# Retention gates and output product: 512- and 256-column matmuls into two banks instead of three 256-column matmuls into one

## The chip, the cores and the metric

The kernel runs on one core of a Trainium2 chip. A core has a matrix engine (TensorE, in the profile PE, with PEld for its weight loads), a vector engine (VectorE, DVE), an activation engine (ScalarE, ACT), a general engine (GpSimd, POOL) and a queue that starts transfers (SyncE, SP). Each engine runs its instructions in the order in which they were written out for it, and waits on semaphores for the others. The metric is the device time of one execution in microseconds (us). Three runs of the kernel before gave 1389.72, 1392.71 and 1392.83 us, median 1392.71.

## The reference

A trunk of four layers works on 256 frames of 1024 channels in float32. Layers 0 and 3 mix the frames by retention, layer 1 by a convolution module, layer 2 by stick-breaking attention; each layer ends with a squared-ReLU feed-forward network. The change touches the second half of the retention mixer, which is this (four heads, 512 value channels each):

```python
proj = xn @ w_in
q, k, v, g = jnp.split(proj, [D_MODEL, 2 * D_MODEL, 4 * D_MODEL], axis=-1)
...
y = (y - mu) * lax.rsqrt(var + EPS)
y = y * gn_w + gn_b
return (jax.nn.silu(g) * y) @ w_out
```

The gate g is a 1024 x 2048 product, w_out a 2048 x 1024 one. Both appear in layers 0 and 3.

## The kernel before, in words

**Numbers.** Float32 products are made from two parts: a value is the sum of hi and lo, and a product is taken as hi x hi + hi x lo + lo x hi. Activations lie transposed (channels on the 128 partitions), as tiles of 128 x 512 whose columns 0 to 255 are hi and 256 to 511 lo (S is 256). Helper `split` (L349, L350) makes such a tile: a cast gives hi, a VectorE subtraction gives lo. x itself is kept as four tiles x0 to x3 of 128 x 512.

**Weights.** They stream in as units of 128 x 1024, in the order in which the program uses them. ScalarE casts a unit to `wh` (L337), VectorE subtracts to get `wl` (L338). There are five buffers of each kind, so a unit is cast only when the unit five before it has been used for the last time. A unit holds eight weight tiles of 128 x 128: four contraction steps (kk) times two halves of the output (m).

**Two ways to multiply.** `mm_b` (L457 to L459) issues three matmuls of 256 columns for each weight tile (wh x hi, wh x lo, wl x hi), all into one half of one PSUM bank; two output halves share a bank. `mm_w` (L484, L485) issues one matmul of 512 columns (wh x [hi, lo]) and one of 256 (wl x hi) into a bank of its own for each half. The bank then holds two sums that must still be added: `sum_w` copies one half to SBUF on ScalarE (L507) and adds the other on VectorE (L508). The accumulators `acc` have four banks, and four other banks, `mis`, serve everything small; a tile takes the bank that was free first.

**The retention part.** For each head: the y product into two `mis` banks (L793 to L796), squares on ScalarE (L800), sums on GpSimd, a column sum on TensorE (L374), and a reciprocal root on two columns on VectorE, which gives G. Two gate pairs p = 0, 1 follow (L818): `pair_b` with two units each, a multiplication by the norm's factor (L820) and a SiLU (L822). G is spread over partitions by a TensorE product, `bcast` (L381), copied out of its bank by ScalarE (L385, Gb). Then y is finished for each half e: VectorE multiplies by Gb (L828), ScalarE applies scale and bias twice (L833), VectorE multiplies by the SiLU (L838), and two splits (L349, L350) give two tiles of the output product's input. A scheduler that simulates the engines fixes each engine's order, so that the steps of one head stand among the matmuls of the next.

**The output product.** `res_pairs` computes four output pairs in two groups of two. For each of four contraction units kb (one head each) and each pair it uses one unit; after the last unit a pair is added to x by one VectorE instruction (L851), and its norm parts follow (L404, L405, L415). Group 0 needs head 3's y at its last unit.

## Time and profile before

| what | value |
| --- | --- |
| median of three runs | 1392.71 us (1389.72 to 1392.83) |
| the profiled execution | 1390.83 us |
| its span | 1389.0 us, so 1.83 us lie outside it |
| TensorE busy | 1371.8 us, 8838 matmuls |
| VectorE, ScalarE, GpSimd busy | 1011.7, 794.9, 190.6 us |
| gates of layer 0, output product of layer 0 | 109 to 163 us, 163 to 211 us |
| the same in layer 3 | 1094 to about 1148 us, and on to about 1203 us |

A matmul's row gives its start and its modelled length. Matmuls overlap, so the step from one start to the next says what a matmul costs, and the length does not. The clock of TensorE stands in the column PEclk, 1.00 being full speed.

### The profile page before, as it was taken

To read this page: it belongs to the slowest core of one execution; us is meant where nothing else is said; L and a number is where in the kernel's file an instruction comes from. 1 tells how busy PE (TensorE), PEld (TensorE's weight loads), DVE (VectorE), ACT (ScalarE), POOL (GpSimd) and SP (SyncE) were. 2 spreads that over 40 slices of the span, in tenths; PEclk is the share of its full clock that TensorE was granted. 3 is DMA by queue.
4 is the path that set the end of the run, shared out by engine and by line. 5 is a ranking of instruction groups with operands and counts; after the bars stand their busy time and mean duration, and the time that the engine had idled before them with its cause. 6 is when DMAs were issued, how large, how long until landed. Compare 5 with 4: busy or idle time off the path is not lost.

```text
span 1389.0 us, 22290 instructions
## 1 busy us (share of the span) xinstructions
PE 1371.8 (99%) x8838; PEld 1244.6 (90%) x8838; DVE 1011.7 (73%) x1715; ACT 794.9 (57%) x1203; POOL 190.6 (14%) x189
## 2 busy tenths in 40 slices
PE   9999999999998999999999999999999999999998
PEld 7889998888998888888988898888988999988888
DVE  6967778775779978766578578755597687788643
ACT  7545556664457556654458666654565554555442
POOL 2201102000449820000000010000110010100011
PEclk9999999999999999999999999999999999999999
DMA  8644445555454035555553345555554444555550
GB/s 302 213 166 149 152 158 198 194 183 186 178 182 152 1 109 195 183 186 194 195 176 128 118 155 186 196 195 182 182 182 175 159 151 155 180 184 186 192 193 35
DMA packets 34522, 235.79 MB, mean 170 GB/s; under 512 B 3952, under 2 KB 4592, under 8 KB 6768
## 3 DMA queue, kind: packets, MB, share of 16 engines
q1 hardware_dynamic: 34128, 233.83, 47.3%
q8 instruction: 69, 1.13, 0.3%
q10 hardware_dynamic: 288, 0.52, 0.1%
q14 instruction: 37, 0.30, 0.1%
HBM read 233.29 MB, written 1.05 MB: 169 GB/s over the span
## 4 chain that ended last, share of the span: by engine, by line
PE 95%; DVE 2%; DMA 1%; ACT 1%; issue 0%; POOL 0%; SPq 0%; ACTq 0%; DVEq 0%; POOLq 0%
PE acc L484 31%; PE acc L485 16%; PE acc L459 9%; PE acc L458 9%; PE acc L457 9%; PE acc L874 4%; PE acc L873 4%; PE acc L875 4%; PE acc L969 2%; PE mis L374 1%; DMA raw<-in_w 1%; PE mis L381 1%; DVE wl L338 1%; PE acc L473 1%; PE acc L472 1%; PE acc L471 1%
## 5 line engine op out<-in xcount | busy, mean ns | idle before, releaser
L338 DVE TENSOR_TENSOR wl<-raw,wh 128x1024 fp32r<-128x1024 f32 (+1 forms) x444 | 555.5, 1254 | 284.4 <-ACT wh L337 279.1
L337 ACT CAST wh<-raw 128x1024 fp32r<-128x1024 f32 (+1 forms) x444 | 461.8, 1042 | 421.7 <-PE acc L484 203.1
L484 PE MATMUL acc<-z,wh 128*128 128x512 f32 x1120 | 391.1, 394 | 0.0
L485 PE MATMUL acc<-z,wl 128*128 128x256 f32 x1120 | 313.1, 281 | 0.0
L484 PE MATMUL acc<-big,wh 128*128 128x512 f32 x768 | 267.7, 393 | 0.0
L484 PEld LDWEIGHTS acc<-z,wh 128*128 128x128 f32 x1120 | 209.3, 187 | 47.3
L485 PE MATMUL acc<-big,wl 128*128 128x256 f32 x768 | 215.2, 280 | 0.0
L485 PEld LDWEIGHTS acc<-z,wl 128*128 128x128 f32 x1120 | 211.5, 189 | 0.8
L484 PEld LDWEIGHTS acc<-big,wh 128*128 128x128 f32 x768 | 143.8, 187 | 32.6
L458 PE MATMUL acc<-big,wh 128*128 128x256 f32 x576 | 163.2, 284 | 1.0 <-DVE big L350 1.0
L457 PE MATMUL acc<-big,wh 128*128 128x256 f32 x576 | 162.3, 286 | 1.9 <-DVE big L349 1.9
L459 PE MATMUL acc<-big,wl 128*128 128x256 f32 x576 | 163.2, 284 | 0.0
L459 PE MATMUL acc<-z,wl 128*128 128x256 f32 x512 | 145.2, 284 | 0.5 <-DVE wl L338 0.5
L457 PE MATMUL acc<-z,wh 128*128 128x256 f32 x512 | 145.4, 284 | 0.0
L485 PEld LDWEIGHTS acc<-big,wl 128*128 128x128 f32 x768 | 145.1, 189 | 0.0
L458 PE MATMUL acc<-z,wh 128*128 128x256 f32 x512 | 144.9, 283 | 0.0
L420 POOL TENSOR_TENSOR t<-t,t 128x512 f32<-128x512 f32 x25 | 38.7, 1549 | 735.3 <-DVE z L405 456.9
L457 PEld LDWEIGHTS acc<-big,wh 128*128 128x128 f32 x576 | 110.3, 193 | 2.8 <-DVE big L349 2.4
L458 PEld LDWEIGHTS acc<-big,wh 128*128 128x128 f32 x576 | 111.2, 193 | 1.2 <-DVE big L350 1.2
L459 PEld LDWEIGHTS acc<-big,wl 128*128 128x128 f32 x576 | 111.2, 193 | 0.0
L459 PEld LDWEIGHTS acc<-z,wl 128*128 128x128 f32 x512 | 98.1, 192 | 0.7 <-DVE wl L338 0.7
L458 PEld LDWEIGHTS acc<-z,wh 128*128 128x128 f32 x512 | 98.1, 192 | 0.0
(252 smaller groups left out, 1964.7 us busy)
## 6 DMA issues: line engine op xcount, KB each, us to landing
raw<-in_w SPq DMA_DIRECT2D x216, 1024.0 KB, 4.8
raw<-in_w SPq DMA_DIRECT2D x8, 512.0 KB, 8.5
x<-in_x SPq DMA_DIRECT2D x4, 256.0 KB, 6.2
cst<-in_cst SPq DMA_DIRECT2D x4, 192.0 KB, 4.9
cst<-in_cst SPq DMA_DIRECT2D x1, 532.0 KB, 9.5
out<-t SPq DMA_DIRECT2D x2, 256.0 KB, 2.7
out<-t ACTq DMA_DIRECT2D x2, 256.0 KB, 2.9
prm<-in_prm SPq DMA_DIRECT2D x1, 189.5 KB, 9.3
```

What stands on the lines that cost most here:

```text
L337: nc.scalar.copy(hi[:, s], src[:, s])
L338: nc.vector.tensor_sub(lo[:, s], src[:, s], hi[:, s])
L420: (nc.vector if p == 3 and self.quick else nc.gpsimd).tensor_add(a, self.sq, q)
L457: nc.tensor.matmul(o, wh[:, kk, cs], ah, start=st, stop=False, **kw)
L458: nc.tensor.matmul(o, wh[:, kk, cs], al, start=False, stop=False, **kw)
L459: nc.tensor.matmul(o, wl[:, kk, cs], ah, start=False, stop=en, **kw)
L484: nc.tensor.matmul(ps[m], wh[:, kk, cs], a, start=first and kk == 0, stop=False, **kw)
L485: nc.tensor.matmul(ps[m][:, :S], wl[:, kk, cs], a[:, :S], start=False, stop=last and kk == 3, **kw)
L873: nc.tensor.matmul(ps[t], zh[:, s], wh[:, kk], start=k == 0, stop=False, skip_group_check=True)
L874: nc.tensor.matmul(ps[t], zh[:, s], wl[:, kk], start=False, stop=False, skip_group_check=True)
L875: nc.tensor.matmul(ps[t], zl[:, s], wh[:, kk], start=False, stop=k == 7, skip_group_check=True)
L969: nc.tensor.matmul(o, dgs[t, w], tap(t, w), start=first, stop=last, **kw)
```

## The change

Four things are edited; what they do in layers 0 and 3 is the same.

- Gate pairs go from `pair_b` to `pair_w`: two banks a pair, then `sum_w` (two ScalarE copies, two VectorE additions of 128 x 256), and L820's multiplication reads the sum from SBUF.
- `res_pairs` with group 2, which only the retention layers use, goes over to `mm_w` with two banks for each output pair, for all four pairs. A group of two pairs so holds all four `acc` banks, where it held two. The last unit of a pair is issued half by half (`by_m`). Four VectorE additions of 128 x 256 take the place of one of 128 x 512 for each pair.
- `pair_w` issues the unit kb = 7 half by half; only the feed-forward network's second product has so many.
- Temporaries are reused in place, and the high part of the four y splits of a head is cast by ScalarE where VectorE did it.

There are 32 gate units and 32 output units in the two layers, with eight weight tiles each: 512 weight tiles lose one matmul of three.

```diff
--- before.py
+++ after.py
@@ -473,16 +473,15 @@
                 nc.tensor.matmul(o, wl[:, kk, cs], a[:, :S], start=False, stop=last and kk == 3, **kw)
 
 
-    def mm_w(self, ps, w, acts, k0, first, last):
+    def mm_w(self, ps, w, acts, k0, first, last, by_m=False):
         nc = self.nc
         wh, wl = v3(w[0], 4, 256), v3(w[1], 4, 256)
         kw = dict(skip_group_check=True)
-        for kk in range(4):
+        for kk, m in [(kk, m) for m in range(2) for kk in range(4)] if by_m else [(kk, m) for kk in range(4) for m in range(2)]:
             a = acts(k0 + kk)
-            for m in range(2):
-                cs = slice(m * P, (m + 1) * P)
-                nc.tensor.matmul(ps[m], wh[:, kk, cs], a, start=first and kk == 0, stop=False, **kw)
-                nc.tensor.matmul(ps[m][:, :S], wl[:, kk, cs], a[:, :S], start=False, stop=last and kk == 3, **kw)
+            cs = slice(m * P, (m + 1) * P)
+            nc.tensor.matmul(ps[m], wh[:, kk, cs], a, start=first and kk == 0, stop=False, **kw)
+            nc.tensor.matmul(ps[m][:, :S], wl[:, kk, cs], a[:, :S], start=False, stop=last and kk == 3, **kw)
 
     def pair_b(self, name, l, c0, acts, nkb=2):
         ps = self.acc()
@@ -496,7 +495,7 @@
         ps = [self.acc(), self.acc()]
         for kb in range(nkb):
             w = self.unit((name, l, "b", kb, c0))
-            self.mm_w(ps, w, acts, kb * 4, kb == 0, kb == nkb - 1)
+            self.mm_w(ps, w, acts, kb * 4, kb == 0, kb == nkb - 1, by_m=kb == 7)
         return self.sum_w(ps)
 
     def sum_w(self, ps):
@@ -527,15 +526,20 @@
         return [self.sum_w(ps[0]), self.sum_w(ps[1])]
 
     def res_pairs(self, name, l, acts, nkb, group, evac, before=None):
+        wide = group == 2
         for g in range(4 // group):
-            ps = [self.acc() for _ in range(group)]
+            ps = [[self.acc(), self.acc()] if wide else self.acc() for _ in range(group)]
             for kb in range(nkb):
                 if before is not None:
                     before(kb)
                 for p in range(group):
                     w = self.unit((name, l, "b", kb, (g * group + p) * 256))
-                    self.mm_b(ps[p], w, acts, kb * 4, kb == 0, kb == nkb - 1)
-                    if kb == nkb - 1:
+                    last = kb == nkb - 1
+                    if wide:
+                        self.mm_w(ps[p], w, acts, kb * 4, kb == 0, last, by_m=last)
+                    else:
+                        self.mm_b(ps[p], w, acts, kb * 4, kb == 0, last)
+                    if last:
                         evac(g * group + p, ps[p])
 
 
@@ -799,10 +803,10 @@
                 s = self.tmp()
                 nc.scalar.activation(out=s, in_=yb[e], func=AF.Square)
                 sq.append(s)
-            ss = self.tmp()
-            nc.gpsimd.tensor_add(ss, sq[0], sq[1])
-            sh = self.tmp(S)
-            nc.gpsimd.tensor_add(sh, ss[:, :S], ss[:, S:])
+            ss = sq[0]
+            nc.gpsimd.tensor_add(ss, ss, sq[1])
+            sh = ss[:, :S]
+            nc.gpsimd.tensor_add(sh, sh, ss[:, S:])
             vr = self.mis()
             for t in range(2):
                 self.colsum(vr[:, t : t + 1], sh[:, t * P : (t + 1) * P], self.sc(512))
@@ -815,9 +819,8 @@
             nc.vector.tensor_mul(G, rs, fh)
             sg = []
             for p in range(2):
-                ps = self.pair_b("ret_w_in", j, 4 * D + h * DV + p * 256, self.zs)
-                t = self.tmp()
-                nc.vector.tensor_mul(v3(t, 2, S), v3(ps, 2, S), self.b2(rb))
+                t = self.pair_w("ret_w_in", j, 4 * D + h * DV + p * 256, self.zs)
+                nc.vector.tensor_mul(v3(t, 2, S), v3(t, 2, S), self.b2(rb))
                 s = self.bigt()
                 nc.scalar.activation(out=s, in_=t, func=AF.Silu)
                 sg.append(s)
@@ -826,17 +829,15 @@
             for e in range(2):
                 u = self.tmp()
                 nc.vector.tensor_mul(v3(u, 2, S), v3(yb[e], 2, S), self.b2(Gb))
-                a = self.tmp()
                 for f in range(2):
                     cc = h * 4 + e * 2 + f
                     s = slice(f * S, (f + 1) * S)
                     nc.scalar.activation(
-                        out=a[:, s], in_=u[:, s], func=AF.Identity,
+                        out=u[:, s], in_=u[:, s], func=AF.Identity,
                         scale=self.p(("gw", j), cc), bias=self.p(("gb", j), cc),
                     )
-                pr = self.tmp()
-                nc.vector.tensor_mul(pr, a, sg[e])
-                y += [self.split(pr[:, :S], "dve"), self.split(pr[:, S:], "dve")]
+                nc.vector.tensor_mul(u, u, sg[e])
+                y += [self.split(u[:, :S]), self.split(u[:, S:])]
         self.out_proj("ret_w_out", j, y, 4, 2, nxt)
 
     def out_proj(self, name, l, y, nkb, group, nxt, bias=None, before=None):
@@ -847,7 +848,12 @@
 
         def evac(p, ps):
             x = self.x[p]
-            if bias is None:
+            if isinstance(ps, list):
+                for f in range(2):
+                    s = slice(f * S, (f + 1) * S)
+                    for o in (ps[f][:, :S], ps[f][:, S:]):
+                        nc.vector.tensor_add(x[:, s], o, x[:, s])
+            elif bias is None:
                 nc.vector.tensor_add(x, ps, x)
             else:
                 for f in range(2):
```

Line numbers rise by a few after the edit: `mm_w` is L483 and L484 there, `sum_w` L506 and L507, the y product L797 to L800, the squares L804, the multiplications L823, L831 and L839, scale and bias L835, the addition to x L855.

Three places of the engines' orders follow. They are in layer 0; layer 3 has the same pattern.

**VectorE where the output product begins.** `mis_1585` and `mis_1586` (after: `mis_1529`, `mis_1530`) hold head 2's y, Gb its factor; `wl` rows are weight units. Before:

```order
L815 TENSOR_TENSOR G_1627<-vy_1617,fq_777 128x2
L338 TENSOR_TENSOR wl_2078<-raw_2047,wh_2077 128x1024
L338 TENSOR_TENSOR wl_2108<-raw_2105,wh_2107 128x1024
L828 TENSOR_TENSOR t_335_1760<-mis_1585,Gb_1695 128x512
L838 TENSOR_TENSOR t_337_1765<-t_336_1762,big_1690 128x512
L828 TENSOR_TENSOR t_340_1773<-mis_1586,Gb_1695 128x512
```

After:

```order
L819 TENSOR_TENSOR G_1569<-vy_1559,fq_777 128x2
L338 TENSOR_TENSOR wl_1944<-raw_1921,wh_1943 128x1024
L338 TENSOR_TENSOR wl_1966<-raw_1963,wh_1965 128x1024
L831 TENSOR_TENSOR t_327_1680<-mis_1529,Gb_1626 128x512
L831 TENSOR_TENSOR t_330_1691<-mis_1530,Gb_1626 128x512
L507 TENSOR_TENSOR t_349_1788<-acc_1744,t_349_1788 128x256
L507 TENSOR_TENSOR t_349_1788<-acc_1745,t_349_1788 128x256
L507 TENSOR_TENSOR t_360_1845<-acc_1801,t_360_1845 128x256
```

The sums that empty head 3's gate banks (`acc_1744` to `acc_1802`) now stand behind the weight unit and both multiplications of the y before. The output product's first matmul takes the bank of `acc_1744`.

**TensorE at the end of group 0.** `mis_1893` (after: `mis_1796`) is the spread of head 3's G; `acc_1987`, `acc_1988` (after: `acc_1875` to `acc_1878`) are group 0, `acc_2241` is group 1; `big_1968` (after: `big_1858`) is head 3's first y tile. Before:

```order
L459 MATMUL acc_1988<-big_1783,wl_2136 128x256
L381 MATMUL mis_1893<-cst,G_1828 128x128 x2
L457 MATMUL acc_2241<-big_1365,wh_2245 128x256
L458 MATMUL acc_2241<-big_1365,wh_2245 128x256
...
L459 MATMUL acc_2241<-big_1579,wl_2304 128x256
L457 MATMUL acc_2241<-big_1582,wh_2303 128x256
L457 MATMUL acc_1987<-big_1968,wh_2165 128x256
```

After:

```order
L484 MATMUL acc_1875<-big_1696,wl_1966 128x256
L381 MATMUL mis_1796<-cst,G_1742 128x128 x2
L483 MATMUL acc_1876<-big_1696,wh_1965 128x512
L484 MATMUL acc_1876<-big_1696,wl_1966 128x256
...
L483 MATMUL acc_1878<-big_1699,wh_1985 128x512
L484 MATMUL acc_1878<-big_1699,wl_1986 128x256
L483 MATMUL acc_1875<-big_1858,wh_2007 128x512
```

Before, 67 matmuls of group 1 stood between the spread and the first use of head 3's y. Now 22 matmuls of group 0 itself stand there, and group 1 begins only after group 0 has given its banks back.

**ScalarE while head 3's y is finished.** Before:

```order
L337 CAST wh_2303<-raw_2301 128x1024
L385 COPY Gb_1896<-mis_1893 128x256
L833 ACTIVATE t_375_1963<-t_374_1961,prm 128x256 x2
L337 CAST wh_2331<-raw_2301 128x1024
L833 ACTIVATE t_380_1976<-t_379_1974,prm 128x256 x2
```

After:

```order
L337 CAST wh_2079<-raw_2077 128x1024
L385 COPY Gb_1799<-mis_1796 128x256
L337 CAST wh_2099<-raw_2077 128x1024
L835 ACTIVATE t_362_1853<-t_362_1853,prm 128x256 x2
L835 ACTIVATE t_365_1864<-t_365_1864,prm 128x256 x2
L337 CAST wh_2121<-raw_2119 128x1024
L349 CAST big_1858<-t_362_1853 128x256
L349 CAST big_1861<-t_362_1853 128x256
```

Two weight casts, and both scale-and-bias steps, now stand ahead of the first cast of y, which VectorE made before.

## The prediction

> **What bounds the kernel now.** I read the page first, then the chain of waits, then stretches of time around the edited places.
>
> ```profile
> PE 1371.8 (99%) x8838; PEld 1244.6 (90%) x8838; DVE 1011.7 (73%) x1715; ACT 794.9 (57%) x1203; POOL 190.6 (14%) x189
> PE 95%; DVE 2%; DMA 1%; ACT 1%; issue 0%; POOL 0%; SPq 0%; ACTq 0%; DVEq 0%; POOLq 0%
> ```
>
> The first row is busy time by engine, the second the chain that ended last. TensorE sets the time: a matmul less is a gain, and any wait of TensorE is a loss. The view of stretches tells whether the edited parts have slack; its first pair of columns is TensorE's, the one after the last engine (POOL) its clock.
>
> ```profile
> 108.80:163.00 54.20, 54.20 (x458) 54.20 (x457) 40.63 (x83) 27.39 (x38) 6.64 (x6) 1.00 0.40 141
> 163.00:211.40 48.40, 48.40 (x407) 48.40 (x406) 37.62 (x62) 26.02 (x38) 3.93 (x4) 1.00 0.48 172
> 1094.00:1148.00 54.00, 54.00 (x456) 54.00 (x455) 41.05 (x83) 26.91 (x38) 6.69 (x6) 1.00 0.41 145
> 1148.00:1203.00 55.00, 55.00 (x462) 55.00 (x462) 43.15 (x67) 30.08 (x44) 6.57 (x5) 1.00 0.48 172
> ```
>
> Gates and output product of layers 0 and 3 leave TensorE no idle time at all. So the change can't remove a wait there. It can shorten the matmuls, and it can bring waits.
>
> **The gain: 512 weight tiles.** Three stretches that hold one kind of matmul only, or nearly:
>
> ```profile
> 190.00:211.00 21.00, 21.00 (x177) 21.00 (x177) 15.53 (x21) 10.96 (x16) 1.43 (x1) 1.00 0.55 193
> 243.73:261.75 18.02, 18.02 (x106) 15.89 (x105) 13.25 (x25) 12.25 (x20) 0.00 (x0) 1.00 0.52 185
> 1228.00:1350.00 122.00, 122.00 (x693) 105.88 (x692) 85.06 (x133) 61.23 (x85) 6.66 (x5) 1.00 0.53 189
> ```
>
> The count takes in about two matmuls already in flight at the left edge. The first stretch is the old form: 21.00 / 175 = 0.120 us a matmul, 0.360 us a weight tile. The second is the new form: 104 matmuls, 52 pairs, 18.02 / 52 = 0.3465 us. The third is the new form in layer 3: 122 / 345.5 = 0.353 us. So a weight tile gains 7 to 13.5 ns, and 512 of them 3.5 to 6.9 us. I take 10 ns, **5.1 us**.
>
> The Trainium skill, page "TensorE: Matmul & The Clock Gate", section "Wait — 56ns, not 53.3ns?", states back-to-back spacings of N / 2.4 GHz plus some 2.5 ns. By that page an estimate for the old form is 327.5 ns and for the new 325 ns a weight tile, a gain of 1.3 us in all. The trace has 360 ns for the old form, so the rule misses most of what each matmul costs here, and the rows stand in the sum.
>
> **What hides and what doesn't.** ScalarE gets 32 copies (L506) and 32 casts of y more, VectorE 32 additions (L507) for those 32 casts, and 32 small additions to x in place of 8 wide ones; with VectorE at 73% and ScalarE at 57% this costs nothing by itself. Nor do the in-place temporaries and the reordered unit kb = 7, since TensorE has no wait there to lose. What matters is where TensorE waits for a result through engines that run in order. With two banks for a pair all four accumulators are taken, so every pair waits for the sums of the pair before last. In the middle of a head this is covered by a pair's 32 matmuls (16 x 0.3465 = 5.5 us). Three kinds of places aren't covered.
>
> *Places 1 and 2: head 3's first gate pair, and the start of the output product.* Both follow on a spread (L381), a y product of 1.15 us, and in the order of VectorE the needed sum stands behind a weight unit and both multiplications by Gb. The rows of before at the second of these places, each from its engine's timeline (start, length, engine, line):
>
> ```profile
> 161.74 0.60 PE L381 MATMUL mis<-cst,G 128*128 128x128 f32 x4
> 162.68 0.36 PE L793 MATMUL mis<-big,big 128*128 128x256 f32 x1
> 163.25 0.36 PE L457 MATMUL acc<-big,wh 128*128 128x256 f32 x1
> 161.87 1.05 ACT L337 CAST wh<-raw 128x1024 fp32r<-128x1024 f32 x1 [1.82 <-PE acc L458]
> 162.82 0.37 ACT L385 COPY Gb<-mis 128x256 f32<-128x256 f32 x1
> 162.95 1.23 DVE L338 TENSOR_TENSOR wl<-raw,wh 128x1024 fp32r<-128x1024 f32 x1 [1.65 <-ACT wh L337]
> 164.09 0.69 DVE L828 TENSOR_TENSOR t<-mis,Gb 128x512 f32<-128x512 f32 x1
> ```
>
> The cast at 161.87 waits for the weight buffer that the gate pair has just used up, and in the changed order it waits for the same. Count from the spread's start, B = 161.74. The cast holds Gb back to B+1.08, done B+1.45. The weight unit's VectorE part runs B+1.21 to 2.44, the first multiplication starts at B+2.35. The second starts 0.60 later (the spacing 187.00 to 187.60 in the next fence), the addition 0.60 after that, B+3.55. It takes 0.42:
>
> ```profile
> L508 DVE TENSOR_TENSOR t<-acc,t 128x256 f32<-128x256 f32 x166 | 69.1, 419 | 14.4 <-ACT t L507 14.1
> L507 ACT COPY t<-acc 128x256 f32<-128x256 f32 x166 | 60.7, 372 | 56.9 <-PE acc L485 56.6 <-PE acc L526 0.3
> L800 ACT ACTIVATE t<-mis 128x512 f32<-128x512 f32 x16 | 8.8, 585 | 1.1 <-PE mis L796 1.1
> ```
>
> So the bank is free at about B+4.0, where TensorE would be ready at 163.25 = B+1.51: a wait of **2.5 us**. Some 0.55 of it falls earlier, since y's second bank now is the one that the spread used and must wait for Gb's copy (163.19 against 162.68). ScalarE alone would allow little less: second square after that bank, then the copy, done at about B+3.3, and the addition at B+3.7. Behind the addition the scale-and-bias steps, the splits and the root of the next head wait too, but each has over 5 us until its use.
>
> *Place 3: head 3's y at group 0's last unit.* Before, group 1 covered it:
>
> ```profile
> 182.20 0.60 PE L381 MATMUL mis<-cst,G 128*128 128x128 f32 x4
> 183.28 0.37 ACT L385 COPY Gb<-mis 128x256 f32<-128x256 f32 x1
> 185.27 1.09 ACT L833 ACTIVATE t<-t,prm 128x256 f32<-128x256 f32 x2 [1.62 <-DVE t L828]
> 186.27 1.03 ACT L337 CAST wh<-raw 128x1024 fp32r<-128x1024 f32 x1
> 187.00 0.68 DVE L828 TENSOR_TENSOR t<-mis,Gb 128x512 f32<-128x512 f32 x1
> 187.60 0.49 DVE L349 CAST big<-t 128x256 fp32r<-128x256 f32 x2
> 189.14 0.75 DVE L350 TENSOR_TENSOR big<-t,big 128x256 fp32r<-128x256 f32 x2
> 190.56 0.52 PE L457 MATMUL acc<-big,wh 128*128 128x256 f32 x3
> ```
>
> From spread (182.20) to the first finished tile (189.14 + some 0.42) it took 7.4 us, and TensorE came at 190.56, 8.4 us after. After the change TensorE has 0.36 + 11 x 0.3465 = 4.2 us of work in between. Along the new order, from the spread X: Gb done X+1.0; multiplications X+1.0 and X+1.6; a weight cast on ScalarE, X+1.5 to 2.55; scale and bias of both halves up to X+4.5 (two take 1.0); VectorE's L839 X+3.75; another weight cast X+4.45 to 5.5; the cast of y X+5.4 to 5.8; VectorE's weight unit X+5.55 to 6.7, and only then the low part, done X+7.1. TensorE waits until X+7.2: **3.0 us**.
>
> *Place 4: group 1's first bank.* Its last sum goes over three additions of 0.335 us spacing that follow the last four weight tiles; the freeing one ends some 0.25 us after TensorE is ready: **0.3 us**.
>
> The sum a layer is 2.5 + 2.5 + 3.0 + 0.3 = 8.3 us, 16.6 in both. From below: if the sums at places 1 and 2 don't stand behind the products of y, 6.6 remain in all; from above the same plus 2 us for late weight units after a wait (five buffers of 2.8 us cover those, so I leave it out). Head 2's first gate pair has the same queue, but y's second half lies later in the matmuls, and I get TensorE there 0.45 us after its bank; if that cover is gone it costs a few tenths.
>
> **The clock.** A wait of TensorE may cost twice. Rows of TensorE in stretches (busy, then PEclk), and two matmuls:
>
> ```profile
> 40.00:42.00 2.00, 1.20 (x11) 1.00 0.00 0
> 490.00:492.00 2.00, 0.51 (x4) 1.00 0.00 0
> 492.00:494.00 2.00, 1.00 (x8) 1.00 0.00 0
> 494.00:496.00 2.00, 2.00 (x12) 0.52 0.00 0
> 494.42 0.42 PE L458 MATMUL acc<-big,wh 128*128 128x256 f32 x1
> 495.91 0.41 PE L458 MATMUL acc<-big,wh 128*128 128x256 f32 x1
> ```
>
> After 2.5 idle us of four the clock fell to half: seven matmuls in 1.49 us, 0.213 each against 0.120, for some 3.3 us. That loses 3.3 x (1 - 0.120/0.213) = 1.44 us. An idle 0.8 us at 40 left the clock alone. The six waits of 2.5 and 3.0 us lie near the former. None of it to all six is 0 to 8.6 us; I take two, **3 us**.
>
> The same page of the Trainium skill, Part 1, "What's actually happening", has the clock fall only after an idle window of about 3.4 us. By that rule none of these waits would do it; the rows above show a fall after less idle time in a row, which speaks against the rule as stated.
>
> **The sum** against the profiled execution: 1390.83 - 5.1 + 16.6 + 3 = 1405.3. The runs' median lies 1.9 us above that execution and one run 1.1 below; I say **1405.5 us**, 1.0% slower.
>
> **The rivals.**
>
> - *The clock stays.* Then 1390.8 - 5.1 + 16.6 = 1402.3. For it: no wait reaches 3.3 us in one piece. Against: the fall at 494.
> - *The clock falls at every wait.* 1402.3 + 8.6 = 1411. For it: idle shares much like those at 490 to 494. Against: a wait that itself lies in the slow stretch loses nothing.
> - *Only head 3's y is late.* Places 1 and 2 vanish if the sums come ahead of the y products; 1390.8 - 5.1 + 6.6 = 1392.3, no change. For it: copies and sums themselves are short, 0.37 + 0.42 us. Against: the order of VectorE.
> - *Faster: the chains run under TensorE's own work*, as they do at head 2. This decides if the sum comes within 1.5 us of the spread instead of 4.0, and y within 4.2 instead of 7.2. Then only the gain is left, 1384 to 1387. For it: TensorE had no wait here before, with queues as full. Against: both chains are longer than that without any queue.
>
> **How the numbers follow.** Chances: forecast 0.37, clock stays 0.25, clock falls everywhere 0.15, only y late 0.16, faster 0.07. A measurement of this kernel tells about 0.3%, 4.2 us, from no change. Slower takes the first three nearly whole, 0.75; the half case gives nearly all of same, 0.17; faster 0.08. The range, 1392 to 1412, holds from the half case to the clock falling everywhere. Of the first three alone it would be 1400 to 1412.
>
> **What would show it.** Step by step: 512 fewer matmuls, and pairs at 0.347 to 0.353 us in 109 to 211; idle time before `mm_w`'s first line on `acc`, released by VectorE's L507, of about 2 us at four places; idle time of 3 us released by L350 at two; PEclk below 1.00 in the 3 us after. I am wrong if TensorE stays dense from 109 to 220, if the waits end with ScalarE's weight cast, or if pairs in the gates cost 0.36 us after all.

## The result

The changed kernel takes 1410.92 us (median of four runs, 1404.70 to 1411.28), the kernel before, run on the same chip, 1391.51 us (1389.72 to 1392.83): 1.013 times as long, 95% interval 1.0098 to 1.0161. It is slower, as forecast, and inside the range; 1405.5 us was 5.4 too little. The profiled execution took 1411.21 us with a span of 1409.3, before 1390.83 and 1389.0.

The page after, busy time by engine and the chain that ended last:

```profile
PE 1379.0 (98%) x8325; PEld 1222.8 (87%) x8326; DVE 1014.6 (72%) x1739; ACT 815.2 (58%) x1267; POOL 189.0 (13%) x189
PE 93%; DVE 4%; ACT 1%; issue 1%; DMA 0%; POOL 0%; SPq 0%; DVEq 0%; ACTq 0%; POOLq 0%
```

Some 512 matmuls are gone (513 records), and yet TensorE is busy 7 us longer. Its share of the chain that ended last fell by two points, and VectorE's rose by two. The view of TensorE's waits (us in total, times, longest) names what is new:

```profile
PE acc L483 <- DVE t L507: 7.1, 7, 1.4
PE acc L483 <- DVE big L350: 5.5, 2, 2.8
...
PE acc L483 <- DVE x L855: 0.2, 1, 0.2
```

`acc` waits for the sums (L507) seven times, four of them for 1.41 us, and for head 3's y (L350) twice. Neither row is there before. Six of the seven lie in the retention; the last, 0.72 us, is in layer 0's feed-forward network. The retention stretches, dense before, now have idle time in TensorE's first pair of columns (the number after POOL's is the clock):

```profile
112.50:166.28 53.78, 51.99 (x314) 45.54 (x314) 40.54 (x84) 31.29 (x56) 6.49 (x6) 1.00 0.38 137
166.28:215.00 48.72, 44.35 (x255) 38.67 (x254) 34.21 (x59) 27.64 (x46) 3.50 (x3) 0.96 0.43 152
1102.00:1160.00 58.00, 56.23 (x346) 49.77 (x345) 44.68 (x92) 35.54 (x64) 6.56 (x6) 1.00 0.40 141
1160.00:1215.00 55.00, 50.73 (x283) 43.99 (x282) 37.06 (x65) 29.78 (x49) 3.48 (x3) 0.94 0.45 158
```

The idle time is 1.8 and 4.4 us in layer 0, 1.8 and 4.3 in layer 3; in the second stretch of each layer the clock fell too. The spans split at landmarks of TensorE's timeline (first y product, first matmul on `w_out`'s weights, first of the feed-forward network, first of the depthwise convolution, and the same in layer 3). The row of layer 0's feed-forward network so takes in layer 1's first product:

| stretch | before, us | after, us | difference |
| --- | --- | --- | --- |
| start to the first y of layer 0 | 106.47 | 109.34 | +2.87 |
| gates of layer 0 | 56.78 | 61.27 | +4.49 |
| output product of layer 0 | 48.19 | 50.58 | +2.39 |
| feed-forward network of layer 0 | 227.17 | 230.32 | +3.15 |
| on to the first y of layer 3 | 653.49 | 652.41 | -1.08 |
| gates of layer 3 | 56.78 | 60.83 | +4.05 |
| output product of layer 3 | 48.18 | 51.88 | +3.70 |
| rest of layer 3 | 191.99 | 192.62 | +0.63 |
| span | 1389.05 | 1409.25 | +20.20 |

The four retention rows give +14.6; the prediction's terms gave -5.1 + 16.6 + 3 = +14.5. The other 5.6 us lie mostly in two stretches that the prediction left as they were: the start, whose code the change does not touch, and layer 0's feed-forward network, where it only reorders the unit kb = 7.

### The places, row by row

*Place 2, the start of the output product*: TensorE, then ScalarE, then VectorE, each from its timeline after.

```profile
166.28 0.60 PE L381 MATMUL mis<-cst,G 128*128 128x128 f32 x4
166.64 0.36 PE L797 MATMUL mis<-big,big 128*128 128x256 f32 x1
...
168.38 0.36 PE L797 MATMUL mis<-big,big 128*128 128x256 f32 x1
...
170.61 0.50 PE L483 MATMUL acc<-big,wh 128*128 128x512 f32 x1 [1.41 <-DVE t L507]
...
167.31 0.36 ACT L385 COPY Gb<-mis 128x256 f32<-128x256 f32 x1
168.14 0.60 ACT L804 ACTIVATE t<-mis 128x512 f32<-128x512 f32 x1 [0.46 <-PE mis L800]
169.24 0.60 ACT L804 ACTIVATE t<-mis 128x512 f32<-128x512 f32 x1 [0.50 <-PE mis L800]
169.73 1.20 ACT L506 COPY t<-acc 128x256 f32<-128x256 f32 x4
...
168.59 1.28 DVE L831 TENSOR_TENSOR t<-mis,Gb 128x512 f32<-128x512 f32 x2
170.13 1.42 DVE L507 TENSOR_TENSOR t<-acc,t 128x256 f32<-128x256 f32 x4 [0.27 <-ACT t L506]
```

From B = 166.28, the spread, the sum that frees the bank starts at B+3.85 and TensorE goes on at B+4.33. VectorE finishes both products at 169.87 and then idles 0.27 us for ScalarE: the copy L506 stands behind the second square (L804), and that waits for TensorE's own y product. So the last link is ScalarE's queue, with VectorE's 0.3 us earlier.

The loss is not B+4.33 less B+1.51. In the new order both halves of y, four groups from 166.64 to 168.38, follow the spread; before, two groups did (162.10 and 162.68). A group lasts 0.58, so TensorE has work until B + 0.36 + 4 x 0.58 = B+2.68, and place 2 loses 4.33 - 2.68 = 1.65 us. In the same way place 1 loses 1.93 in layer 0, 0.25 of it ahead of y's second half, and the two places of layer 3 lose 1.64 each.

*Place 3, head 3's y at group 0's last unit*, X = 184.08:

```profile
188.29 0.28 PE L484 MATMUL acc<-big,wl 128*128 128x256 f32 x1
191.28 0.77 PE L483 MATMUL acc<-big,wh 128*128 128x512 f32 x1 [2.71 <-DVE big L350]
...
184.72 0.37 ACT L385 COPY Gb<-mis 128x256 f32<-128x256 f32 x1 [1.24 <-PE mis L381]
185.67 1.05 ACT L337 CAST wh<-raw 128x1024 fp32r<-128x1024 f32 x1 [0.57 <-PE acc L483]
186.62 2.08 ACT L835 ACTIVATE t<-t,prm 128x256 f32<-128x256 f32 x4
188.60 1.03 ACT L337 CAST wh<-raw 128x1024 fp32r<-128x1024 f32 x1
189.54 1.32 ACT L349 CAST big<-t 128x256 fp32r<-128x256 f32 x4
...
189.66 1.22 DVE L338 TENSOR_TENSOR wl<-raw,wh 128x1024 fp32r<-128x1024 f32 x1 [0.24 <-ACT wh L337]
190.81 1.09 DVE L350 TENSOR_TENSOR big<-t,big 128x256 fp32r<-128x256 f32 x3
```

Two weight casts on ScalarE and a weight unit on VectorE stand in the chain, as counted; the low part starts at X+6.7, and TensorE at X+7.2. A matmul of 256 columns takes 0.12 us from start to start, so the place loses 191.28 - 188.29 - 0.12 = 2.87 us, and 2.92 in layer 3. After this wait the next pairs come 0.64 us apart instead of 0.35.

*Place 4, and head 2's first gate pair* (which the prediction held covered by 0.45 us) both wait a little, in this order:

```profile
198.91 0.47 PE L483 MATMUL acc<-big,wh 128*128 128x512 f32 x1 [0.25 <-DVE x L855]
...
138.00 0.47 PE L483 MATMUL acc<-z,wh 128*128 128x512 f32 x1 [0.36 <-DVE t L507]
```

### The profile page after: what moved, and what is told of

It is laid out like the page before. It is cut to its first block, busy times and chain, and to the rows that moved or that the text cites. A ratio compares the mean times of both kernels' runs of the same rounds, so it can differ in the third digit from the quotient of the medians.

```text
span 1409.3 us, 21331 instructions
## 1 busy us (share of the span) xinstructions
PE 1379.0 (98%) x8325; PEld 1222.8 (87%) x8326; DVE 1014.6 (72%) x1739; ACT 815.2 (58%) x1267; POOL 189.0 (13%) x189
## 4 chain that ended last, share of the span: by engine, by line
PE 93%; DVE 4%; ACT 1%; issue 1%; DMA 0%; POOL 0%; SPq 0%; DVEq 0%; ACTq 0%; POOLq 0%
PE acc L483 39%; PE acc L484 20%; PE acc L458 4%; PE acc L459 4%; PE acc L457 4%; PE acc L880 4%; PE acc L879 4%; PE acc L881 4%; PE acc L975 2%; PE mis L374 1%; DVE wl L338 1%; DVE mis L963 1%; PE mis L381 1%; PE acc L473 1%; PE acc L472 1%
## 5 line engine op out<-in xcount | busy, mean ns | idle before, releaser
L338 DVE TENSOR_TENSOR wl<-raw,wh 128x1024 fp32r<-128x1024 f32 (+1 forms) x444 | 554.4, 1251 | 309.8 <-ACT wh L337 305.4
L337 ACT CAST wh<-raw 128x1024 fp32r<-128x1024 f32 (+1 forms) x444 | 461.6, 1042 | 432.3 <-PE acc L483 286.4
L483 PE MATMUL acc<-z,wh 128*128 128x512 f32 x1376 | 483.8, 396 | 4.7 <-DVE t L507 4.3
L484 PE MATMUL acc<-z,wl 128*128 128x256 f32 x1376 | 384.2, 281 | 0.0
L483 PE MATMUL acc<-big,wh 128*128 128x512 f32 x1024 | 363.6, 399 | 8.6 <-DVE big L350 5.5
L483 PEld LDWEIGHTS acc<-z,wh 128*128 128x128 f32 x1376 | 257.3, 188 | 64.9 <-DVE t L507 4.2
L484 PE MATMUL acc<-big,wl 128*128 128x256 f32 x1024 | 288.3, 282 | 0.0
L484 PEld LDWEIGHTS acc<-z,wl 128*128 128x128 f32 x1376 | 259.9, 189 | 1.2
L483 PEld LDWEIGHTS acc<-big,wh 128*128 128x128 f32 x1024 | 193.9, 190 | 55.3 <-DVE big L350 6.1
L484 PEld LDWEIGHTS acc<-big,wl 128*128 128x128 f32 x1024 | 195.5, 191 | 0.3
L420 POOL TENSOR_TENSOR t<-t,t 128x512 f32<-128x512 f32 x25 | 38.7, 1548 | 761.6 <-DVE z L405 328.2
L506 ACT COPY t<-acc 128x256 f32<-128x256 f32 x198 | 70.5, 372 | 44.1 <-PE acc L484 42.8
L458 PE MATMUL acc<-big,wh 128*128 128x256 f32 x320 | 90.4, 283 | 1.0 <-DVE big L350 1.0
L457 PE MATMUL acc<-big,wh 128*128 128x256 f32 x320 | 89.9, 284 | 1.2 <-DVE big L349 1.2
L879 PE MATMUL acc<-wh,z 128*128 128x512 f32 x224 | 87.8, 393 | 0.0
L880 PE MATMUL acc<-wl,z 128*128 128x512 f32 x224 | 87.6, 391 | 0.0
L881 PE MATMUL acc<-wh,z 128*128 128x512 f32 x224 | 87.6, 391 | 0.0
L507 DVE TENSOR_TENSOR t<-acc,t 128x256 f32<-128x256 f32 x198 | 80.8, 416 | 7.4 <-ACT t L506 7.3
L457 PE MATMUL acc<-z,wh 128*128 128x256 f32 x256 | 73.0, 287 | 0.0
L458 PE MATMUL acc<-z,wh 128*128 128x256 f32 x256 | 72.8, 286 | 0.0
```

Of the source, the lines that this page charges most:

```text
L337: nc.scalar.copy(hi[:, s], src[:, s])
L338: nc.vector.tensor_sub(lo[:, s], src[:, s], hi[:, s])
L457: nc.tensor.matmul(o, wh[:, kk, cs], ah, start=st, stop=False, **kw)
L458: nc.tensor.matmul(o, wh[:, kk, cs], al, start=False, stop=False, **kw)
L483: nc.tensor.matmul(ps[m], wh[:, kk, cs], a, start=first and kk == 0, stop=False, **kw)
L484: nc.tensor.matmul(ps[m][:, :S], wl[:, kk, cs], a[:, :S], start=False, stop=last and kk == 3, **kw)
```

## The experiments

Retention is the time from the first y product to the feed-forward network (in layer 3, to its first matmul), one layer each; the border between gates and output product moves where the order changes, so their sum is compared. "ffn" is the row of layer 0's feed-forward network above. Medians are of all executions, stage times of the one that was profiled: run 6's (1392.64 us) is the shortest of its ten, run 9's (1392.81) the second longest.

| kernel | median, us | ratio (95%) | first y at | retention, layers 0 and 3 | ffn |
| --- | --- | --- | --- | --- | --- |
| before | 1391.51 | 1 | 106.47 | 104.97, 104.96 | 227.17 |
| after | 1410.92 | 1.013 (1.0098 to 1.0161) | 109.34 | 111.85, 112.71 | 230.32 |
| 1 gates only | 1399.06 | 1.0043 (1.0028 to 1.0058) | 106.88 | 108.32, 107.91 | 227.17 |
| 2 output only | 1403.67 | 1.0079 (1.0064 to 1.0094) | 106.26 | 109.12, 109.33 | 230.13 |
| 3 own temporaries | 1431.92 | 1.0274 (1.0254 to 1.0295) | 114.10 | 119.31, 119.48 | 230.14 |
| 4 the same, group 0 narrow | 1406.01 | 1.0099 (1.0082 to 1.0116) | 112.88 | 108.07, 108.05 | 227.20 |
| 5 wait filled | 1405.32 | 1.0107 (1.0079 to 1.0135) | 106.73 | 110.66, 110.20 | 230.23 |
| 6 gates only, own temporaries | 1396.26 | 1.0030 (1.0017 to 1.0042) | 106.84 | 105.44, 105.44 | 228.45 |
| 7 the same and group 1 wide | 1403.80 | 1.0087 (1.0062 to 1.0111) | 109.66 | 109.58, 108.07 | 230.05 |
| 8 only group 1 wide | 1394.55 | 1.0018 (1.0007 to 1.0030) | 109.59 | 104.53, 104.53 | 230.09 |
| 9 neither product wide | 1390.16 | 0.9992 (0.9982 to 1.0002) | 109.35 | 104.96, 104.96 | 227.18 |
| 10 before, group 1 wide | 1390.97 | 0.9997 (0.9985 to 1.0009) | 109.21 | 105.49, 105.71 | 226.99 |
| 11 as 6, y cast on VectorE | 1391.70 | 1.0000 (0.9990 to 1.0011) | 109.16 | 103.73, 103.73 | 228.45 |
| 12 after, once more | 1409.01 (one run) | | 109.55 | 112.06, 110.25 | 230.28 |

### 1 and 2: each half of the change alone

Run 1 keeps the gates of the change and gives the output product its old form; run 2 the other way round.

```diff
-        wide = group == 2
+        wide = False
```

> The change with its output product put back to the old form (mm_b, one bank for a pair); the gates keep two banks. My theory: the loss is made of waits at single places, and the waits at head 3's first gate pair and at the output product's start (2.8 to 3.1 us each, two a layer, 11.5 us in all) belong to the gates; head 3's y is covered again by group 1. So 1391.5 + 11.5 - 2.6 (256 weight tiles at 10 ns) = about 1400, with four waits of some 1.4 us on the sums' line and none of 2.8 on the splits. Rival, the loss is a general one (the sums and copies load VectorE and ScalarE, spread over the whole region): half of the loss too, about 1401, but with the waits spread over many matmuls. Rival, the clock falls are the main thing: without the 2.8 us waits they go, and the time is 1393 to 1396.

```diff
-                t = self.pair_w("ret_w_in", j, 4 * D + h * DV + p * 256, self.zs)
-                nc.vector.tensor_mul(v3(t, 2, S), v3(t, 2, S), self.b2(rb))
+                ps = self.pair_b("ret_w_in", j, 4 * D + h * DV + p * 256, self.zs)
+                t = self.tmp()
+                nc.vector.tensor_mul(v3(t, 2, S), v3(ps, 2, S), self.b2(rb))
```

> The change with its gates put back to the old form (pair_b, one bank); the output product keeps two banks a pair for all four pairs. My theory: only head 3's y is late, 2.9 us of work lost in each layer, with a clock fall of 1.5 to 2.7 us after it: 1391.5 + 5.7 + 3 to 5 - 2.6 = 1398 to 1400, and the two waits of about 2.8 us on the splits' line stand in the profile. Rival, the loss lies with banks and sums in general: the waits on the gates' side vanish, and with half of the sums gone it is half of the whole loss or less, without waits on the splits.

TensorE's waits of run 1, then of run 2:

```profile
PE acc L483 <- DVE t L507: 3.5, 4, 1.4
...
PE acc L457 <- DVE t L507: 2.8, 2, 1.4
```

```profile
PE acc L483 <- DVE big L350: 7.7, 2, 3.9
```

Run 1 has the waits for the sums and none for y in the output product; its four long ones are places 1 and 2 of both layers (place 2 is now the old form's L457). In the retention run 2 has places 3 alone, 3.9 us each: y's chain from the spread to TensorE takes 6.95 us there, about as in the whole change, but TensorE has work for 2.9 us of it, not 4.3. That is 1 us a place more than was expected. So each half is slower by itself, +6.4 and +11.0 us against 1392.65 us, and their retention stretches add up to the whole: 3.35 + 2.95 and 4.15 + 4.37, 14.8 us beside 14.6. That only head 3's y is late, the rival near no change, falls with run 1.

### 3, 4, 6 and 7: sums out of the shared temporaries

The sums of a gate pair took their temporary from the pool that the squares and products of y use as well. Here they have two of their own.

```diff
-        self.t2 = pool("t2", 10)
+        self.t2 = pool("t2", 8)
...
-        o = self.tmp()
+        o = self.t2.tile([P, 512], F32, name=self.nm("gt"), tag="gt", bufs=2) if own else self.tmp()
```

> The whole change, but the gate sums get two temporaries of their own (the shared pool goes from ten to eight, so memory is the same). In the order of VectorE the sums then stand ahead of the products of the head before. My theory: the sums were late because the shared temporaries are given out in program order, behind those of the head before, and not because two banks are too few. Then the four waits at head 3's first gate pair and the output product's start vanish, and 11.5 us of the loss: 1410.9 - 11.5 = about 1399.5, with head 3's two waits of 2.8 us left. Rival, four banks are too few for pairs of two: the waits stay, 1408 to 1411. Rival, the clock falls are the main thing: they stay with the 2.8 us waits, 1405 or more.

```profile
PE acc L483 <- DVE big L350: 15.8, 4, 4.4
PE mis L374 <- POOL t L428: 6.1, 1, 6.1
PE mis L381 <- DVE G L819: 6.1, 2, 3.0
```

The view of TensorE's waits of run 3 has no wait of 1.4 us for a sum any more. But now others come late: G, whose reciprocal root is taken on VectorE (twice, 3.0 us each), and y, on which TensorE waits twice in each layer. The total is the worst of all, 32 us above what was expected. Part of that has nothing to do with the retention: with two temporaries fewer, the wait at L374 at the kernel's start grew to 6.1 us, and the first y came at 114.10. Run 4 narrows group 0 on top of this, runs 6 and 7 leave ten temporaries and take two buffers from another pool:

```diff
-        wide = group == 2
         for g in range(4 // group):
+            wide = group == 2 and g == 1
```

> As the run before it, and only the last two output pairs (group 1) use 512 and 256 columns; group 0 keeps the old form with one bank a pair, so that group 1's first pair can run while head 3's y is finished. 384 weight tiles keep the gain. My theory: no wait is left, and the time is 1391.5 - 3.8 = 1387.7, faster than before by 0.3%. Rival, head 3's y is late in this order too, since group 1's first pair now has only a few matmuls between the spread and the first use: 1391.5 - 3.8 + 5 or more, 1393 or above. Rival, a general load of VectorE and ScalarE: 1394 or above without any long wait.

```diff
-        self.big = pool("big", 36)
+        self.big = pool("big", 34)
...
-        wide = group == 2
+        wide = False
```

> Gates with two banks and temporaries of their own for the sums, the output product in its old form; the shared pool keeps its ten tiles (two tiles less in the pool of 36 instead), since the run with eight had a wait of 5 to 6 us at the start of the program where the kernel before has 0.9. My theory: with the sums ahead of the products no wait is left at head 3's first gate pair and the output product's start, and the wait at the start is gone: 1391.5 - 2.6 = 1389, faster than the gates run by 10 us. Rival, the sums then push the products back, and head 3's y or G comes late: 1392 to 1397 with waits on the splits' or the spread's line. Rival, the wait at the start comes from the sums' own tiles: 1396 or above.

Run 7 is run 6 with group 1 wide (`wide = group == 2 and g == 1`).

> As the run before it, and the last two output pairs with 512 and 256 columns. Measured against the same kernel with eight shared temporaries (1406.0), this tells what the wait at the start cost. My theory: 5 us of wait and about 2 of clock, so 1399, with the small waits in the output product (0.3 to 1.2 us on casts and splits, 3.5 us a layer) left. Rival, the shared pool has nothing to do with the start: 1405 to 1407 again.

With the gates alone (run 6) TensorE is dense where run 1 was not; two stretches of run 6 and, behind them, one of run 1:

```profile
108.00:162.00 54.00, 54.00 (x339) 1.00 0.42 151
1096.00:1150.00 54.00, 54.00 (x339) 1.00 0.43 153
```

```profile
109.00:163.00 54.00, 52.21 (x316) 1.00 0.38 135
```

Retention falls from 108.3 to 105.4 us. In VectorE's order the sum of the pair before now stands ahead of the two products of y (at head 3's first gate pair of layer 0 its two halves start at 146.85 and 148.94, the products at 149.27). Run 3, which leaves the pool `big` alone, loses the same waits. That shows the cause of places 1 and 2: where the sums stand in the order, which their temporaries' pool decides. It still isn't below before's 104.97, because y is now late by small amounts, 0.33 us a layer behind a cast (L349) and 0.84 behind a low part (L350). Of these three waits for L350 one is another layer's:

```profile
PE acc L458 <- DVE big L350: 2.7, 3, 1.0
```

With group 1 wide as well (runs 4 and 7) a layer takes 2.6 to 4.1 us more than in run 6, so the gates' gain and group 1's don't add: TensorE also waits for a weight unit's two parts (L337 up to 1.2 us, L338 0.5) and for one more cast of y (0.6), and in layer 0 of run 7 the clock falls behind them. Runs 4, 6 and 7 were each expected faster than they are, by 18, 7 and 5 us.

### 11: what is left in run 6

The cast of y's high part goes back from ScalarE to VectorE.

```diff
-                y += [self.split(u[:, :S]), self.split(u[:, S:])]
+                y += [self.split(u[:, :S], "dve"), self.split(u[:, S:], "dve")]
```

> As the gates run with temporaries of their own (1396.3), with the y casts back on VectorE as in the kernel before. That run has waits of 0.3 and 0.8 us a layer on y's casts and splits. Theory: the casts wait on ScalarE behind scale and bias and a weight cast, so on VectorE they come earlier and the waits go: 2.4 us less, 1394. Rival, the waits come from the sums that were put ahead: no difference, 1396.

The same row of the view of waits has only the other layer's wait left:

```profile
PE acc L458 <- DVE big L350: 1.0, 1, 1.0
```

Retention is 103.73 us in both layers, 1.24 less than before. This is the gain itself, laid bare: 1.24 us for the 128 weight tiles of a layer's gates is 9.7 ns each. The total, 1391.7, is before's all the same: 2.5 us gained here stand against a later start of the first y (109.16) and 1.3 us more in the row of the feed-forward network, of which 0.93 is one wait (L374 for L420) that runs 6 and 7 have too.

### 8, 9 and 10: the output product's second group, and the small edits

Run 8 is run 2 with group 0 narrow. Run 9 has both products in the old form, so what is left of the change are the temporaries used in place, the casts on ScalarE and the unit kb = 7 half by half. Run 10 is before with nothing but group 1 wide.

```diff
-        wide = group == 2
         for g in range(4 // group):
+            wide = group == 2 and g == 1
```

> Gates in the old form, only the last two output pairs with 512 and 256 columns. 128 weight tiles keep the gain, 1.3 us. My theory: the output product's loss comes from group 0 holding all four banks, so with group 0 narrow the long waits go; small ones on casts, as in the run with own temporaries, may stay, up to 3 us a layer: 1390 to 1396, against 1403.7 with all four pairs wide. Rival, any wide pair in the output product brings a wait of 3 to 4 us at head 3's y: 1400 or above.

```diff
-        wide = group == 2
+        wide = False
```

> Gates and output product both in the old form; what is left of the change are the temporaries reused in place, the y casts on ScalarE and the order of the unit kb = 7. My prediction had these at nothing: 1391 to 1393, and 56.8 us from the first y product to the output product in each layer, as before. Rival, they cost something on their own: the two runs with old gates had 58.0 us there, so 1.2 us a layer, 1393 to 1395.

```diff
-            ps = [self.acc() for _ in range(group)]
+            wide = group == 2 and g == 1
+            ps = [[self.acc(), self.acc()] if wide else self.acc() for _ in range(group)]
```

> The kernel before with one thing changed: the last two output pairs use 512 and 256 columns (and the unit kb = 7 its order); temporaries and casts as before. 128 weight tiles at 10 ns: 1391.5 - 1.3 = 1390 if no wait comes with it; a version that might beat the kernel before, though by less than these runs can tell. If the feed-forward network of layer 0 takes the slower of its two paces (0.353 us a pair for 0.347), as in the run with gates in the old form and these two pairs wide, 3 us more: 1393.

Run 9 is before again, in its total and in its retention (104.96): the small edits cost nothing. Run 10 was expected to gain 1.3 us and does not: TensorE waits 0.98 us in each layer for the low part of head 3's y (L350), and retention is 0.5 and 0.7 us longer than before. Run 8, whose casts of y are on ScalarE, has no such wait. Run 8 has no wait in the retention at all:

```profile
109.00:160.00 51.00, 51.00 (x430) 1.00 0.41 146
160.00:214.00 54.00, 54.00 (x393) 1.00 0.51 176
```

So the 3.9 us of run 2 come from group 0 holding all four banks, by which group 1 can no longer cover y. Group 1 alone gains 0.43 us a layer over run 9, 64 weight tiles, 6.7 ns each. And yet run 8 is 4.4 us slower than run 9 in the median; 2.9 of that lie in the feed-forward network behind it, which is the same code in both, and 0.44 of that is a wait for a sum.

### 5 and 12: the clock

Before group 0's last unit, 12 matmuls of ones go into a spare bank, whose result nothing uses. They end about when head 3's y is there, and so fill the wait.

```diff
+                if wide and g == 0 and kb == nkb - 1:
+                    self.warm(12)
```

> The whole change, with twelve matmuls of ones (512 columns, bf16, into a spare bank, result unused) at the place where TensorE waits for head 3's y; they fill 2.6 of its 2.9 us and change nothing else. My theory: the clock falls because TensorE stands idle there, and costs 1.5 us in layer 0 and 2.7 in layer 3. Then the clock stays at 1.00 after the wait and the time drops by about 4 us, 1410.9 to 1407. Rival, the fall is not tied to this wait (it comes by chance of a free-running window, or from the waits before): PEclk still goes to 0.5 near it, and the time stays at 1409 to 1412. A third way: the matmuls of ones start late and delay the first product, then the time rises by up to 2.6 us a layer.

The changed kernel was then run once more as it is.

> The changed kernel once more, unchanged, to see what differs between two profiles of one program. Its first profile reached the first y product at 109.3 us, the kernel before at 106.5, in code that the change does not touch, with a clock fall at 44 to 48; the run with ones has the same code there and reached it at 106.7. Theory: that part is chance, 106.3 to 109.7 again; the four waits of 1.4 us, the two of 2.8 and the pace of layer 0's feed-forward network (0.353 us a pair) come back to within 0.1 us, and the clock falls after the 2.8 us waits again, for 3 to 6 us. Rival, the clock falls by chance alone: it stays at 1.00 after at least one of the two.

TensorE from 192 in layer 0 and from 1186 in layer 3 (busy, clock): after, run 12, and run 5 at its own times.

```profile
192.00:198.00 6.00, 6.00 (x29) 0.77 0.04 15
1186.00:1192.00 6.00, 6.00 (x22) 0.55 0.04 16
```

```profile
192.00:198.00 6.00, 6.00 (x28) 0.74 0.06 23
1186.00:1192.00 6.00, 5.88 (x33) 1.00 0.12 51
```

```profile
186.00:192.00 6.00, 5.89 (x31) 1.00 0.51 179
192.00:198.00 6.00, 5.77 (x33) 1.00 0.12 16
1182.00:1188.00 6.00, 5.75 (x33) 1.00 0.07 30
```

With the wait filled the clock stays at 1.00, and the output products are 1.2 and 2.5 us shorter (50.58 to 49.39, 51.88 to 49.34). So this is what the clock costs at place 3. Run 12 bears it out without any filling: in layer 3 the clock did not fall, after a wait of the same 2.76 us, and the output product took 49.44.

Why one wait brings the clock down and its like does not can be read from when falls begin. Within each of the fourteen traces all falls begin whole multiples of 3.413 us apart (in after at 191.33 and 1184.61, 291 of them), and a fall lasts whole windows too: in after one in layer 0 and two in layer 3. The windows around layer 3's place 3, after and then run 12:

```profile
1181.20:1184.61 3.41, 1.35 (x8) 1.00 0.39 118
1184.61:1188.02 3.41, 2.71 (x8) 0.50 0.45 190
```

```profile
1181.57:1184.99 3.42, 1.57 (x10) 1.00 0.36 101
1184.99:1188.40 3.41, 2.49 (x14) 1.00 0.51 216
```

The same wait left 2.06 us of a window idle in after, and a fall followed; in run 12 the border of a window cut it into 1.84 and 0.92, and none did. In all traces, past the first 60 us, a fall followed every window with over 1.9 us idle, and some of those with 1.6 to 1.9. Idle time is not all of it (in run 7 a window with 0.93 us idle sufficed, from 403.98). Where the windows lie differed between these two executions of one kernel, so whether a wait of this length brings the clock down is chance.

The profile of run 5, 6.5 us shorter than the changed kernel's, holds another 2.6 us of a first y at 106.73 instead of 109.34, and that code is the same in both.

### The feed-forward network of layer 0

Most kernels take 227.0 to 227.2 us for it or 230.1 to 230.3, and run 9, which differs from before there only in the order of the unit kb = 7, belongs to the first. (Runs 6 and 11, at 228.45, and run 7, at 230.05, have the wait of 0.93 us in it, run 7 also a fall of the clock; all three have the faster pace.) One stretch in the middle of it, before and after:

```profile
280.00:320.00 40.00, 40.00 (x233) 1.00 0.55 189
```

```profile
280.00:320.00 40.00, 40.00 (x229) 1.00 0.54 185
```

TensorE is dense at full clock in both, but after fits two pairs fewer into 40 us. Run 9 has 233 matmuls there like before, run 12 has 229 like after. From start to start, 43 pairs of before at 270 to 285 us have a mean of 0.3467 us, 42 of after 0.3533. It is the same in run 12 as in after, and goes with the kernel, not with the execution: 0.3467 in before and in 1, 4, 6, 7, 9, 10, 11, and 0.3533 in after and in 2, 3, 5, 8, 12. What sets it isn't known. One thing goes with it in all fourteen traces: the six kernels of the slower pace, and no other, have a wait of TensorE for a sum (L507) early in this network, 0.72 us in after, 0.44 in run 8. It is not shown to be the cause; in layer 3 before and run 9 have the slower pace without any such wait. Of the 3.15 us between after and before 0.9 have come up by the 120th of the 448 pairs, around that wait, and 2.2 more by the end, from the pace.

## Why the prediction was right, step by step

**The bound** held: TensorE, with dense stretches in which a wait can only be added.

**The gain, 5.1 us for 512 tiles.** Runs 11 and 8 measure 9.7 ns a tile in the gates and 6.7 ns in group 1; 10 ns was taken. By the spacings of the Trainium skill, page "TensorE: Matmul & The Clock Gate", section "Wait — 56ns, not 53.3ns?", it would be 2.5 ns, which both runs speak against. (For the old form that rule gives 327.5 of the 360 ns measured: it is short by a tenth, and does not miss "most of what each matmul costs", as the prediction put it.) Group 0's part could not be seen apart from its wait. Taken like group 1's, 256 tiles at 9.7 and 256 at 6.7 ns make 4.2 us.

**Places 1 and 2, 2.5 us each, 10 in all: mis-sized.** They measure 1.93 and 1.65 in layer 0 and 1.64 twice in layer 3, 6.9 in all. The step that failed is "TensorE would be ready at 163.25 = B+1.51": it took TensorE's rows from before, where half of y follows the spread, for an order in which all of it does. A second error went the other way: the bank came free at B+4.3 to 4.6 and not B+4.0, because the second half's square ran later and the copy stood behind it on ScalarE. The sentence that ScalarE alone would allow little less was the one that decided. Runs 1 and 6 show the mechanism.

**Place 3, 3.0 us: right**, 2.87 and 2.92 measured, and in layer 0 each step of its chain to within some 0.1 us. Runs 2 and 8 show the cause.

**Place 4, 0.3 us: right**, 0.41 and 0.27 from start to start. **Head 2's cover** of 0.45 us was gone in both layers, as the prediction allowed for, at 0.52 us each from start to start.

**The clock, 3 us for two of six waits.** It fell at place 3 only. By run 5 it cost 1.2 and 2.5, 3.7 us in all; the fall in layer 3 lasted two windows. That there were two in this execution is chance: run 12 has one. That it would stay is refuted by after's 192 to 198, that it falls at every wait by the waits at places 1 and 2: the stretches 112.5 to 166.28 and 1102 to 1160, which hold place 1, stand at 1.00, and the matmul after place 2's wait has a length of 0.50 us where the one after place 3's has 0.77.

The same page of the Trainium skill, Part 1, "What's actually happening", ties the fall to an idle window of about 3.4 us. Here it came after 2.7 us in one piece, and after another such wait it didn't. Read as a wait of that length, as the prediction reads it, the rule would have missed 3.7 us; the rows show windows of that length, of which 2.06 us idle were enough.

**The small edits at nothing: right** (run 9). **The rival that both chains run under TensorE's own work** falls with the waits: the bank comes free at B+4.3 with work until B+2.7, y at X+7.2 with work until X+4.3.

**The sum.** -4.2 + 6.9 + 5.8 + 0.7 + 1.0 + 3.7 = 13.9 by the measured sizes, beside 14.6 measured and 14.5 predicted; 0.7 us are not assigned. So that the sum agrees to 0.1 us is luck: 3 us too much at places 1 and 2, and as much too little in the gain (0.9), at head 2 (1.0), for the clock (0.7) and in what is not assigned.

**What was not in it** lies by the profiles mostly in two stretches, 3.15 us in the feed-forward network and 2.87 at the start; between forecast and median are 5.4. The pace goes with the kernel and not with one of the edits: all kernels with the slower pace have the output product wide at least in group 1, but 4, 7 and 10 have that too, and the faster pace. The late start begins with a wait that already stood in before, here of after, with the stretch behind it, and then of before:

```profile
43.51 0.60 PE L374 MATMUL mis<-cst,t 128*128 128x1 f32 x4 [1.63 <-POOL t L428]
...
44.00:46.00 2.00, 2.00 (x14) 0.64 0.72 295
```

```profile
42.13 0.61 PE L374 MATMUL mis<-cst,t 128*128 128x1 f32 x4 [0.93 <-POOL t L428]
...
44.00:46.00 2.00, 2.00 (x19) 1.00 0.95 392
```

0.7 us more of waiting, and then a slow clock. All nine traces with such a fall between 44 and 48 us have their first y at 109.16 or later, the five without at 106.88 or earlier. Run 5 has after's code there and the early start; runs 9 and 11 have the late one and are no slower than before. Whether chance or the kernel's layout decides it is open: the changed kernel had it in both its profiles.

No version beat the kernel before: 9, 10 and 11 lie within 0.1% of it, with intervals that hold 1.

## What to carry to other kernels

A form of work that is cheaper by 10 ns a tile pays for few waits, 5 us for 512 tiles here: one bank more for each result takes away the cover that lets the results be finished, and here four waits of under 2 us and two of 3 ate three times the gain. Count TensorE's own work behind a wait in the new order, not in the old trace. Where helpers share a pool of temporaries, the pool, too, sets the order in which engines serve each other; give the temporaries that free a bank a pool of their own, and look at what then comes late instead.

## What was not expected of the hardware

- The same pair of matmuls, 512 and 256 columns at full clock without idle time, steps by 0.3467 us in some stretches and 0.3533 in others, steadily over hundreds of pairs and the same in both profiles of the changed kernel. It is worth 2.2 us here, nearly half of the gain looked for.
- The clock of TensorE fell to half after a wait of 2.71 us and after one of 2.76, and not after another of 2.76; four waits of 1.41 us left it alone. Falls begin on a grid of 3.413 us that runs through the whole execution, and how much of one window is idle decides most of them here. In the pairs 0.64 us apart that follow, some 1.5 us are lost over five pairs in layer 0 and 2.7 over nine in layer 3. Matmuls whose result nobody uses, put into the wait, keep it up.
